# Forget gates as 16 more columns of the first query, key and value projection, h written out tile by tile, and the gate bias on GpSimd's queue

## The chip, the cores and the metric

The kernel runs on one core of a Trainium2 chip. A core has TensorE (PE in the profile; its weight loads are PEld), VectorE (DVE), ScalarE (ACT), GpSimd (POOL) and SyncE (SP, which here only issues DMAs). Each engine works through its own list of instructions in a fixed order; an instruction that has to wait for another engine or for a DMA holds up everything behind it on its engine. The metric is the device time of one execution in microseconds (us).

## The reference, cut to what matters

The program is a decoder trunk for 1024 positions and 1024 features in fp32. It runs a state space layer, a gated feed-forward block, an attention layer, a second feed-forward block and a last norm. The change touches the way into the attention layer:

```python
hn = rmsnorm(h, mix_norm_g[1])
proj = hn @ w_in                       # 1024 x (4*1024 + 16)
q = rmsnorm(proj[..., 0:1024].reshape(.., 16, 64), q_norm_g)
k = rmsnorm(proj[..., 1024:2048].reshape(.., 16, 64), k_norm_g)
v = proj[..., 2048:3072].reshape(.., 16, 64)
gate = proj[..., 3072:4096]
log_f = log_sigmoid(proj[..., 4096:] + b_f)     # 16 columns, one per head
cum = cumsum(log_f over positions)
sc = q @ k^T / 8 + cum[i] - cum[j], causal      # softmax, times v
h = h + (o * sigmoid(gate)) @ w_out
```

## The kernel before, in words

Every fp32 product is three matmuls of split operands (`mm3`, L45 to L51: high times high, high times low, low times high). `split` (L54) makes the two parts: ScalarE copies the high part (L56), then VectorE subtracts it and writes the low part (L57). So a weight goes DMA, tile `raw`, ScalarE, VectorE, and only then can TensorE use all of it. The tile `raw` has two buffers for the whole program (`bufs=2`). A load takes them in turn, and its DMA can't be issued until both halves of the split two loads earlier have read the buffer.

The layer's input is the norm `Norm`. The output projection of the first feed-forward block finishes the eight tiles of h (128 positions each) one after the other (L591 adds the last part to h), and `Norm.tile` scales each to `hn` (squares on ScalarE L173, the factor on VectorE and GpSimd, the scaling on VectorE L200). After four tiles `turn` transposes them: four transposes per 128 features on TensorE (L213) into a PSUM bank, then the high part on ScalarE (L224, into `xh`) and the low part on VectorE (L225, into `xl`). The first half of the positions is turned while the feed-forward block is still running; the second half in `x.finish(bank)` (L952) at the start of `fox`, with three PSUM banks in turn (two named `mt`, one `pv`).

`fox` then does, for heads in 8 pairs:

- It stores all h tiles to DRAM (L953, L954), since the attention needs their memory; they come back for the output projection.
- The forget gates: the last 128 columns of `w_in` go into `raw` (one DMA), the last 32 of them are split (`split_narrow`), and `proj_narrow` (L99, L103) computes them transposed, 32 matmuls 512 columns wide whose weights are the gate columns. ScalarE copies the result (L1156), TensorE transposes it back (L1158, eight times), and VectorE adds the bias `nbf` (L1165, L1167). The bias comes by a DMA on SP's queue (L1149).
- Pair 0's weights: `qkv_w(0)` issues loads 0, 1 and 2, each a `raw` tile that is split into `wqh` and `wql`. Loads 0 and 1 are two DMAs each (L1001, L1002), load 2 is one (L999).
- `softplus` (L904 to L923: three ScalarE operations with two loads of ScalarE's tables, eight VectorE operations) and the running sum over the position tiles (L1173, seven times).
- `in_qkv` for pair 0: for each of 8 position tiles 24 matmuls, 192 in all, 384 columns wide (128 for each of two heads' q with k, and v), evicted by ScalarE (L1019) and split.
- The sums over positions (L1177, L1178), eight transposes of them (L1185), and `fill` for both heads of pair 0, which transposes q and k (L1063) and writes them out with four ScalarE (L1065 to L1068) and two VectorE operations (L1069, L1071) each, four times. The gate projection of pair 0 and the q, k, v projection of pair 1 are handed out beside that.
- The first scores (L1085 to L1089), whose exponential is L1095 on ScalarE; then the loop over pairs, where `fillers` deals out the next pair's projections as work for TensorE between the scores.

The lists are ordered by a scheduler at build time from what the program says and from when tiles become free, and are fixed from then on. `wqh` and `wql` lie in memory that tiles of the norm and of h held before.

Of the kernel before, what the change touches and what calls it, by code (L numbers as in the profile page):

```python
# [17 lines left out]
P = 128  # L18
S = 1024
D = 1024  # L20
# [159 lines left out]
class Norm:  # L180

    def __init__(self, tc, cx, g):
        self.tc, self.cx, self.g = tc, cx, g
# [10 lines left out]
    def tile(self, t, psum):  # L196
        nc, cx = self.tc.nc, self.cx
        hn_t = self.pool.tile([P, D], F32, name="hn")
        r = rstd_of(self.tc, cx, self.small, cx.h[t], hn_t, D, "n")
        nc.vector.tensor_scalar(out=hn_t, in0=cx.h[t], scalar1=r, scalar2=None, op0=ALU.mult)  # L200
        self.hn.append(hn_t)
        if t == 3:
            self.turn(0, psum)
# [36 lines left out]
class BlockNorm(Norm):  # L240
# [3 lines left out]
    def __init__(self, tc, cx, g, h_dram):  # L244
        super().__init__(tc, cx, None)
        self.h_dram = h_dram
        self.gb = self.pool.tile([P, D], F32, name="gb", bufs=1)
        tc.nc.gpsimd.dma_start(out=self.gb, in_=g.unsqueeze(0).broadcast_to([P, D]))
# [685 lines left out]
def fox(tc, cx, x, w_in, b_f, q_norm_g, k_norm_g, w_out, then):  # L934
# [7 lines left out]
    xh, xl = x.xh, x.xl  # L942
    h_dram = [cx.dram.tile([P, D], F32, name=f"h_dram{t}") for t in range(NT)]
    o_dram = [cx.dram.tile([P, S], F32, name=f"o_dram{p}") for p in range(NPR)]

    with ExitStack() as pst:
# [5 lines left out]
        x.finish(bank)  # L952
        for t in range(NT):  # L953
            nc.sync.dma_start(out=h_dram[t], in_=cx.h[t])  # L954
        cx.close_h()
# [32 lines left out]
        def qkv_w(p):  # L988


            wh = qp.tile([P, KD, 3 * P], F32R, name="wqh")
            wl = qp.tile([P, KD, 3 * P], F32R, name="wql")

# [12 lines left out]

        def in_qkv(w, res):

            wh, wl = w
            vt = sp.tile([P, NT, 2, 2, HD], F32R, name="vt", bufs=2)  # L1010
            qn = []
            for t in range(NT):
                hf, tc_ = t // 4, slice((t % 4) * P, (t % 4 + 1) * P)
                ps = ip_ps([P, 3 * P])
                for k in range(KD):
# [13 lines left out]
                eng.tensor_tensor(out=q_, in0=q_, in1=r.unsqueeze(2).broadcast_to([P, 4, HD]), op=ALU.mult)  # L1029
                qn.append(q_.rearrange("p a d -> p (a d)"))  # L1030
            res.update(qn=qn, vt=vt)

# [115 lines left out]
        nbf = sp.tile([P, FH], F32, name="nbf")  # L1148
        nc.sync.dma_start(out=nbf, in_=b_f.broadcast_to([P, FH]))  # L1149
        wf = split_narrow(nc, cx, load_raw(nc, cx, win[:, :, f0:f0 + P]))  # L1150
        fps = small_ps([P, NT, 2, NARROW])
        for hf in range(2):
            ps = ip_ps([P, HF])
            proj_narrow(nc, ps, wf, xh[hf], xl[hf])
            raw = ap_.tile([2 * NARROW, HF], F32, name="ph", bufs=BP)
            nc.scalar.activation(out=raw, in_=ps[0:2 * NARROW], func=AF.Copy)  # L1156
            for c in range(4):
                nc.tensor.transpose(out=fps[:, hf * 4 + c].rearrange("p a h -> p (a h)"), in_=raw[:, c * P:(c + 1) * P],  # L1158
                                    identity=cx.ident[0:2 * NARROW, 0:2 * NARROW])
        res = {}  # L1160
        w, loads = qkv_w(0)
        for f in loads:
            f()
        v = ap_.tile([P, NT, FH], F32, name="g", bufs=1)
        nc.vector.scalar_tensor_tensor(out=v, in0=fps[:, :, 0, FH:2 * FH], scalar=-1.0,  # L1165
                                       in1=nbf.unsqueeze(1).broadcast_to([P, NT, FH]), op0=ALU.mult, op1=ALU.subtract)
        nc.vector.tensor_tensor(out=v, in0=v, in1=fps[:, :, 1, FH:2 * FH], op=ALU.subtract)  # L1167
        sv = ap_.tile([P, NT, FH], F32, name="pl", bufs=BP)
# [158 lines left out]
def trunk_kernel(ctx, tc, x, mix_norm_g, ffn_norm_g,  # L1327
# [4 lines left out]

    def norm(name):
        return lambda: Norm(tc, cx, cx.cols[name])

    def blocks(i):
        return lambda: BlockNorm(tc, cx, ffn_norm_g[i], [cx.dram.tile([P, D], F32, name=f"hf_{i}_{t}") for t in range(NT)])

# [10 lines left out]
    n = ssd(tc, cx, n, ssd_w_in[0], ssd_dt_bias, ssd_a_log, ssd_d, ssd_w_out[0], blocks(0))  # L1349
    n = ffn(tc, cx, 0, n, ffn_w_up, ffn_w_down, norm("mix1"))  # L1350
    n = fox(tc, cx, n, fox_w_in[0], fox_b_f, fox_q_norm_g, fox_k_norm_g, fox_w_out[0], blocks(1))
# [30 lines left out]
```

## Time and profile before

| | us |
|---|---|
| median of 3 runs | 2848.11 (2844.68 to 2848.8) |
| the profiled execution | 2847.88 |
| its span | 2846.2 |
| TensorE busy in it | 2789.2 (98%) |
| VectorE, ScalarE, GpSimd busy | 1983.6, 1439.3, 241.6 |
| mean granted clock of TensorE | 0.998 of full speed |

The span is the time from the first to the last instruction that the profiler saw; 1.7 us of the profiled time lie around it. The stretch in question runs from 1440.5 us (the feed-forward block's last matmul) to about 1511 us (the second scores) of the span. Matmuls overlap, so TensorE's time per matmul is the distance of two starts, not the duration that a row shows.

### The profile page before, as it was taken

What the parts mean: (1) busy time and instruction counts of PE and PEld (TensorE: products, weight loads), DVE (VectorE), ACT (ScalarE), POOL (GpSimd) and SP (SyncE); (2) the same over time, 40 slices, a digit from 0 to 9 for tenths busy, and PEclk for the clock granted to TensorE, in tenths of its full rate; (3) what the DMA queues carried; (4) which work ended last, traced back from release to release, by engine and by line L of the source; (5) the groups of instructions that cost most, each with busy time, mean ns of one, the idle gap of its engine ahead of it and who ended that gap; (6) DMA issues with size and microseconds to landing.
All of it is one profiled execution on the core that took longest, in us unless ns stands there. A gap on an engine that the chain in (4) does not pass through costs nothing. (4 is left out here: it accounts for less than half of the span.)

```text
span 2846.2 us, 37033 instructions
## 1 busy us (share of the span) xinstructions
PE 2789.2 (98%) x14083; PEld 2323.0 (82%) x14083; DVE 1983.6 (70%) x3159; ACT 1439.3 (51%) x2371; POOL 241.6 (8%) x281
## 2 busy tenths in 40 slices
PE   8999999999999999999999999999999999999998
PEld 6888888888778888888888888888877888888887
DVE  6667666666777677667656777776687876776765
ACT  5753754646544444444436666666553544444334
POOL 1000000000100000000023222222200000000000
PEclk9999999999999999999999999999999999999999
DMA  4221212212223333386421111111142233334952
GB/s 138 68 75 52 67 52 64 77 38 75 82 96 97 99 109 104 104 301 207 135 69 29 31 38 38 38 38 38 34 139 102 87 110 111 104 104 138 331 157 103
DMA packets 263394, 275.92 MB, mean 97 GB/s; under 512 B 44162, under 2 KB 193734, under 8 KB 263216
## 3 DMA queue, kind: packets, MB, share of 16 engines
q1 hardware_dynamic: 262448, 271.81, 29.9%
q8 instruction: 111, 1.82, 0.3%
q0 software_dynamic: 752, 1.74, 0.2%
q14 instruction: 67, 0.55, 0.1%
q10 hardware_dynamic: 16, 0.00, 0.0%
HBM read 212.04 MB, written 61.47 MB: 96 GB/s over the span
## 5 line engine op out<-in xcount | busy, mean ns | idle before, releaser
L56 ACT ACTIVATE wh<-raw 128x1024 fp32r<-128x1024 f32 (+2 forms) x162 | 150.2, 929 | 383.0 <-PE fp L50 222.8
L49 PE MATMUL fp<-xh,wh 128*128 128x512 f32 x704 | 274.9, 390 | 0.4 <-DVE h L1318 0.4
L50 PE MATMUL fp<-xl,wh 128*128 128x512 f32 x704 | 274.5, 390 | 0.0
L51 PE MATMUL fp<-xh,wl 128*128 128x512 f32 x704 | 274.3, 390 | 0.0
L57 DVE TENSOR_TENSOR wl<-raw,wh 128x1024 fp32r<-128x1024 f32 (+1 forms) x160 | 171.2, 1070 | 133.8 <-ACT wh L56 133.8
L50 PE MATMUL ip<-xl,wh 128*128 128x512 f32 x640 | 254.8, 398 | 0.0
L49 PE MATMUL ip<-xh,wh 128*128 128x512 f32 x640 | 254.3, 397 | 0.0
L51 PE MATMUL ip<-xh,wl 128*128 128x512 f32 x640 | 253.5, 396 | 0.0
L50 PE MATMUL fp<-wl,ah 128*128 128x512 f32 x616 | 240.5, 390 | 1.0 <-DVE wl L57 0.7
L51 PE MATMUL fp<-wh,al 128*128 128x512 f32 x616 | 239.8, 389 | 0.0
L49 PE MATMUL fp<-wh,ah 128*128 128x512 f32 x616 | 239.0, 390 | 0.0
L478 DVE TENSOR_TENSOR g<-g,fp 128x512 f32<-128x512 f32 x132 | 90.6, 687 | 167.2 <-PE fp L51 167.2
L49 PE MATMUL ip<-wqh,xh 128*128 128x384 f32 x512 | 183.2, 359 | 0.6 <-ACT wqh L56 0.6
L50 PE MATMUL ip<-wql,xh 128*128 128x384 f32 x512 | 174.6, 341 | 1.3 <-DVE wql L57 1.3
L51 PE MATMUL ip<-wqh,xl 128*128 128x384 f32 x512 | 172.9, 338 | 0.0
L56 ACT ACTIVATE ah<-ra 128x1024 fp32r<-128x1024 f32 x84 | 82.6, 988 | 173.7 <-PE fp L50 147.5
L56 ACT ACTIVATE wh<-s 128x1024 fp32r<-128x1024 f32 x88 | 93.5, 1062 | 123.9 <-PE fp L50 120.7
L49 PEld LDWEIGHTS fp<-xh,wh 128*128 128x128 f32 x704 | 132.5, 188 | 27.9 <-ACT wh L56 0.6
L50 PEld LDWEIGHTS fp<-xl,wh 128*128 128x128 f32 x704 | 132.5, 188 | 27.5
L51 PEld LDWEIGHTS fp<-xh,wl 128*128 128x128 f32 x704 | 132.4, 188 | 27.4
L475 ACT ACTIVATE g<-fp 128x512 f32<-128x512 f32 x176 | 103.1, 586 | 101.1 <-PE fp L51 101.1
L694 DVE SCALAR_TENSOR_TENSOR xs<-ip,col,xs 128x511 f32<-128x511 f32 (+2 forms) x120 | 89.1, 745 | 74.1 <-ACT xs L689 73.2
(362 smaller groups left out, 7057.1 us busy)
## 6 DMA issues: line engine op xcount, KB each, us to landing
raw<-in_ffn_w_up_dram SPq DMA_DIRECT2D x88, 512.0 KB, 3.8
a_S<-g SPq DMA_DIRECT2D x88, 256.0 KB, 2.0
raw<-in_ssd_w_in_dram SPq DMA_DIRECT2D x41, 512.0 KB, 3.9
ra<-a_S SPq DMA_DIRECT2D x40, 512.0 KB, 5.9
a_A<-a SPq DMA_DIRECT2D x66, 256.0 KB, 2.1
m<-acs_dram SPq DMA_DIRECT2D x64, 256.0 KB, 3.4
raw<-in_ffn_w_down_dram SPq DMA_DIRECT2D x30, 512.0 KB, 4.9
ra<-a_A SPq DMA_DIRECT2D x30, 512.0 KB, 4.1
```

What stands on the lines that cost most here:

```text
L49: nc.tensor.matmul(out=out, lhsT=lh, rhs=rh, start=start, stop=False, **kw)
L50: nc.tensor.matmul(out=out, lhsT=lh, rhs=rl, start=False, stop=False, **kw)
L51: nc.tensor.matmul(out=out, lhsT=ll, rhs=rh, start=False, stop=stop, **kw)
L56: nc.scalar.activation(out=hi, in_=src, func=AF.Copy)
L57: nc.vector.tensor_tensor(out=lo, in0=src, in1=hi.bitcast(F32), op=ALU.subtract)
L475: nc.scalar.activation(out=to, in_=p, func=AF.Copy)
L478: nc.vector.tensor_tensor(out=to, in0=to, in1=p, op=ALU.add)
L694: nc.vector.scalar_tensor_tensor(out=a[:, sh:], in0=ps[:, 0:HF - sh], scalar=wt, in1=a[:, sh:], op0=ALU.mult, op1=ALU.add)
```

## The change

1. `Norm` gets the DRAM tiles for h and stores each tile of h inside `Norm.tile`, as the feed-forward blocks' norm already did. The loop that stored all eight after `x.finish` is gone.
2. The forget gates have no projection of their own any more. `wqh` and `wql` are 16 columns wider. The same `raw` tile with the last 128 columns of `w_in` is loaded, its last 16 columns are split into columns 384 to 399 of pair 0's `wqh` and `wql`, and then loads 0 to 2 follow. `in_qkv` of pair 0 runs with `more=16`: its 192 matmuls are 400 columns wide, and per position tile one VectorE operation (L1032) adds the bias to the 16 columns. `softplus` and the running sums stand behind `in_qkv` of pair 0 instead of ahead of it. The 32 narrow matmuls, the eight transposes and the two ScalarE copies go.
3. The bias `nbf` is loaded on GpSimd's queue instead of SP's.

```diff
 class Norm, tile():
+        if self.h_dram is not None:
+            nc.sync.dma_start(out=self.h_dram[t], in_=cx.h[t])
 fox():
         x.finish(bank)
-        for t in range(NT):
-            nc.sync.dma_start(out=h_dram[t], in_=cx.h[t])
...
-            wh = qp.tile([P, KD, 3 * P], F32R, name="wqh")
-            wl = qp.tile([P, KD, 3 * P], F32R, name="wql")
+            wh = qp.tile([P, KD, 3 * P + FH], F32R, name="wqh")
+            wl = qp.tile([P, KD, 3 * P + FH], F32R, name="wql")
...
-        def in_qkv(w, res):
+        def in_qkv(w, res, more=0):
-            wh, wl = w
+            wh, wl = (part[:, :, 0:3 * P + more] for part in w)
-                ps = ip_ps([P, 3 * P])
+                ps = ip_ps([P, 3 * P + more])
...
+                if more:
+                    nc.vector.scalar_tensor_tensor(out=res["more"][:, t], in0=ps[:, 3 * P:3 * P + more], scalar=-1.0,
+                                                   in1=nbf, op0=ALU.mult, op1=ALU.subtract)
...
-        nc.sync.dma_start(out=nbf, in_=b_f.broadcast_to([P, FH]))
-        wf = split_narrow(nc, cx, load_raw(nc, cx, win[:, :, f0:f0 + P]))
-        fps = small_ps([P, NT, 2, NARROW])
-        for hf in range(2):
-            ps = ip_ps([P, HF])
-            proj_narrow(nc, ps, wf, xh[hf], xl[hf])
...
+        nc.gpsimd.dma_start(out=nbf, in_=b_f.broadcast_to([P, FH]))
         res = {}
         w, loads = qkv_w(0)
+        raw = load_raw(nc, cx, win[:, :, f0:f0 + P])[:, :, P - FH:P]
+        split(nc, w[0][:, :, 3 * P:3 * P + FH], w[1][:, :, 3 * P:3 * P + FH], raw)
         for f in loads:
             f()
-        v = ap_.tile([P, NT, FH], F32, name="g", bufs=1)
...
+        v = res["more"] = ap_.tile([P, NT, FH], F32, name="g", bufs=1)
+        for _ in in_qkv(w, res, FH):
+            pass
         softplus(...)
         running sums (...)
-        for _ in in_qkv(w, res):
-            pass
```

The lists of the engines are the same up to the second half's turn and again from pair 1's scores on. Three places in between follow. In these rows `mt`, `pv` and `ip` are PSUM tiles, and the waits name the engine or the DMA ring that releases the instruction.

The first place is ScalarE's list at the turn of the second half. Before, the split of load 0 (`wqh<-raw` 128x8x128) stands behind three of the eight evictions, and the narrow columns of the forget gates were split still earlier:

```order
L224 ACTIVATE xh_11446<-mt,col_679 128x512 [waits PE_49] x2
L224 ACTIVATE xh_11446<-pv,col_679 128x512 [waits PE_49]
L56 ACTIVATE wqh<-raw 128x8x128 [waits DMAHW3_49,DMAHW2_49,DMAHW1_49]
L224 ACTIVATE xh_11446<-mt,col_679 128x512 [waits PE_49] x2
L224 ACTIVATE xh_11446<-pv,col_679 128x512 [waits PE_49]
L1156 ACTIVATE ph<-ip 64x512 [waits PE_49]
L56 ACTIVATE wqh<-raw 128x8x128 [waits DMAHW6_49,DMAHW5_49]
```

Now all eight evictions come first (the last rows of them are shown), then the 16 columns and the three loads in a row:

```order
L226 ACTIVATE xh_11454<-pv,col_679 128x512 [waits PE_49]
L226 ACTIVATE xh_11454<-mt,col_679 128x512 [waits PE_49] x2
L56 ACTIVATE wqh<-raw 128x8x16 [waits DMAHW2_49,DMAHW3_49,DMAHW1_49,DVE_49]
L56 ACTIVATE wqh<-raw 128x8x128
L56 ACTIVATE wqh<-raw 128x8x128 [waits DMAHW2_49,DMAHW1_49]
L56 ACTIVATE wqh<-raw 128x8x128 [waits DMAHW3_49]
```

The split that frees the forget gates' `raw` buffer, and the split of load 0, moved behind the last eviction; VectorE's list changed in the same way, with four small operations ahead of the split.

The second place is SP's list. Before, load 1 of pair 0 (L1001, L1002) is issued between the stores of h:

```order
L954 DMA h_dram_11430<-h_9832 128x1024 [waits DVE_49]
L1001 DMA raw<-in_fox_w_in_dram 128x8x64 [waits DMAHW5_49,DVE_49]
L1002 DMA raw<-in_fox_w_in_dram 128x8x64 [waits DMAHW6_49]
L954 DMA h_dram_11431<-h_9833 128x1024 [waits DMAHW7_49,DVE_49]
```

Now it stands behind the last store, and load 2 (L998) directly behind it:

```order
L202 DMA hf_mix_6768<-h_9844 128x1024 [waits DMAHW0_49,DVE_49]
L1000 DMA raw<-in_fox_w_in_dram 128x8x64 [waits DMAHW1_49,DVE_49]
L1001 DMA raw<-in_fox_w_in_dram 128x8x64 [waits DMAHW2_49]
L998 DMA raw<-in_fox_w_in_dram 128x8x128 [waits DMAHW3_49,DVE_49]
```

The stores of h keep their places; what moved is load 1, from between them to behind them, with a wait for VectorE. The bias's DMA left the list.

The third place is TensorE's list where pair 0's projection begins. Before, the transposes of the turn have narrow matmuls (L99, L103) between them, and these go on up to the projection:

```order
L99 MATMUL ip<-xh_11446,wh 64x512 [waits Activation_49]
L1158 MATMUL mt<-ident,ph 128x64 [waits DVE_49]
L1158 MATMUL mt<-ident,ph 128x64 x3
L103 MATMUL ip<-xl_11447,wh 32x512
L49 MATMUL ip<-wqh,xh_11211 128x384 [waits Activation_49]
L49 MATMUL ip<-wqh,xh_11211 128x384
L103 MATMUL ip<-xl_11447,wh 32x512 [waits DVE_49]
```

Now the transposes stand alone and the projection follows them directly:

```order
L215 MATMUL mt<-ident,hn 128x128 [waits DVE_49]
L215 MATMUL mt<-ident,hn 128x128 x3
L49 MATMUL ip<-wqh,xh_11223 128x400 [waits Activation_49]
L49 MATMUL ip<-wqh,xh_11223 128x400 x2
L50 MATMUL ip<-wql,xh_11223 128x400 [waits DVE_49]
```

Nothing stands between the last transposes and the first matmuls that wait for `wqh` and `wql`. Further on, the gate projection of pair 0 (24 matmuls 512 wide) now follows pair 0's projection without a break, and the position sums (L1170, L1171), their transposes (L1178) and the `fill` transposes (L1066) stand among the first matmuls of pair 1's projection, where they stood ahead of and inside the gate projection. Ahead of the second scores (L1085, now L1088, into 128x256) stand 72 of pair 1's 192 matmuls, where 42 stood before; all 24 of the gate projection stand ahead of them in both.

## Rows read from the trace of the kernel before

**Rows 1.** The page's first part: busy time, share of the span, instructions.
```profile
PE 2789.2 (98%) x14083; PEld 2323.0 (82%) x14083; DVE 1983.6 (70%) x3159; ACT 1439.3 (51%) x2371; POOL 241.6 (8%) x281
```

**Rows 2.** Windows: stretch, length; busy PE, PEld, DVE, ACT, POOL; clock, DMA share, GB/s.
```profile
1440.50:1456.20 15.70, 13.29 (x76) 8.14 (x74) 12.15 (x21) 10.10 (x18) 2.49 (x5) 1.00 0.41 127
...
1489.60:1512.00 22.40, 18.67 (x105) 15.33 (x104) 15.03 (x27) 19.03 (x31) 6.80 (x4) 1.00 0.31 71
```

**Rows 3.** Timeline of PE: start, us, engine, line, tiles, shapes, count, [idle before].
```profile
1443.17 0.39 PE L99 MATMUL ip<-xh,wh 128*64 128x512 f32 x1
1443.40 0.40 PE L103 MATMUL ip<-xl,wh 128*32 128x512 f32 x1
...
1455.81 0.46 PE L1158 MATMUL mt<-ident,ph 64*128 64x64 f32 x4 [0.68 <-ACT ph L1156]
1456.20 0.45 PE L49 MATMUL ip<-wqh,xh 128*128 128x384 f32 x1
...
1489.07 0.34 PE L51 MATMUL ip<-wqh,xl 128*128 128x384 f32 x1
```

**Rows 4.** Timeline of ACT at the second half's turn and behind it.
```profile
1444.73 1.27 ACT L224 ACTIVATE xh<-mt,col 128x512 fp32r<-128x512 f32 x2 [2.08 <-PE mt L213]
...
1452.94 1.06 ACT L56 ACTIVATE wqh<-raw 128x1024 fp32r<-128x1024 f32 x1 [1.14 <-DMA raw<-in_fox_w_in_dram]
```

**Rows 5.** Timeline of DVE from the first half's turn to the running sums.
```profile
1420.45 5.35 DVE L225 SCALAR_TENSOR_TENSOR xl<-fp,col,xh 128x512 fp32r<-128x512 f32 x8
...
1433.06 0.42 DVE L57 TENSOR_TENSOR wh<-raw,wh 128x256 fp32r<-128x256 f32 x1 [4.49 <-ACT wh L56]
...
1445.45 1.41 DVE L225 SCALAR_TENSOR_TENSOR xl<-mt,col,xh 128x512 fp32r<-128x512 f32 x2 [1.14 <-ACT xh L224]
...
1454.50 1.23 DVE L57 TENSOR_TENSOR wql<-raw,wqh 128x1024 fp32r<-128x1024 f32 x1
...
1463.81 2.17 DVE L1173 TENSOR_TENSOR pl<-pl 128x16 f32<-128x16 f32 x7
```

**Rows 6.** Timeline of SP's queue: when loads 1 and 2 are issued.
```profile
1433.51 0.38 SPq L1001 DMA_DIRECT2D raw<-in_fox_w_in_dram  x1
1433.94 0.58 SPq L1002 DMA_DIRECT2D raw<-in_fox_w_in_dram  x1
...
1448.80 0.38 SPq L999 DMA_DIRECT2D raw<-in_fox_w_in_dram  x1
```

**Rows 7.** Line L1002's DMAs: time from issue to landing.
```profile
DMA to landing us min/median/max: 3.8/3.9/5.3
```

**Rows 8.** Timeline of ACT behind pair 0's projection.
```profile
1489.44 0.38 ACT L1019 ACTIVATE qn<-ip 128x256 f32<-128x256 f32 x1 [3.61 <-PE ip L51]
...
1489.88 2.01 ACT L56 ACTIVATE wqh<-raw 128x1024 fp32r<-128x1024 f32 x2
1491.78 1.07 ACT L56 ACTIVATE k<-mt 32x512 fp32r<-32x512 f32 x2
...
1496.34 1.06 ACT L56 ACTIVATE wqh<-raw 128x1024 fp32r<-128x1024 f32 x1 [0.87 <-DMA raw<-in_fox_w_in_dram]
1497.63 0.68 ACT L1065 ACTIVATE q<-mt,gqk 64x512 fp32r<-64x512 f32 x1 [0.23 <-PE mt L1063]
...
1508.80 1.28 ACT L1095 ACT_TABLE_LOAD   x1
1510.10 0.37 ACT L1095 ACTIVATE e<-sc,mx 128x128 f32<-128x128 f32 x1
```

**Rows 9.** Timeline of PE at pair 1's first matmuls and the second scores.
```profile
1498.72 0.45 PE L50 MATMUL ip<-wql,xh 128*128 128x384 f32 x1
...
1510.61 0.39 PE L1085 MATMUL sc<-k,q 128*128 128x256 f32 x1 [2.14 <-ACT e L1095]
```

**Rows 10.** Windows near the span's start, columns as in rows 2.
```profile
21.00:23.00 2.00, 1.28 (x10) 0.92 (x10) 1.55 (x3) 2.00 (x6) 1.33 (x2) 1.00 0.00 0
...
25.00:27.00 2.00, 2.00 (x8) 1.48 (x7) 1.87 (x3) 1.79 (x4) 0.00 (x0) 0.50 0.04 11
27.00:29.00 2.00, 2.00 (x11) 1.51 (x10) 1.65 (x3) 1.40 (x4) 0.00 (x0) 0.70 0.93 251
```

More of the change, by code (lines that the diff above doesn't have):

```diff
@@ L180, with __init__ @@
 class Norm:
-    def __init__(self, tc, cx, g):
-        self.tc, self.cx, self.g = tc, cx, g
+    def __init__(self, tc, cx, g, h_dram=None):
+        self.tc, self.cx, self.g, self.h_dram = tc, cx, g, h_dram
         self.st = ExitStack()
@@ L244, in __init__ @@
     def __init__(self, tc, cx, g, h_dram):
-        super().__init__(tc, cx, None)
-        self.h_dram = h_dram
+        super().__init__(tc, cx, None, h_dram)
         self.gb = self.pool.tile([P, D], F32, name="gb", bufs=1)
@@ L942, in fox @@
     xh, xl = x.xh, x.xl
-    h_dram = [cx.dram.tile([P, D], F32, name=f"h_dram{t}") for t in range(NT)]
+    h_dram = x.h_dram
     o_dram = [cx.dram.tile([P, S], F32, name=f"o_dram{p}") for p in range(NPR)]
@@ L1148, in fox @@
         nbf = sp.tile([P, FH], F32, name="nbf")
-        nc.sync.dma_start(out=nbf, in_=b_f.broadcast_to([P, FH]))
-        wf = split_narrow(nc, cx, load_raw(nc, cx, win[:, :, f0:f0 + P]))
-        fps = small_ps([P, NT, 2, NARROW])
-        for hf in range(2):
-            ps = ip_ps([P, HF])
-            proj_narrow(nc, ps, wf, xh[hf], xl[hf])
[L1155 to L1159, printed above, removed]
+        nc.gpsimd.dma_start(out=nbf, in_=b_f.broadcast_to([P, FH]))
         res = {}
         w, loads = qkv_w(0)
+        raw = load_raw(nc, cx, win[:, :, f0:f0 + P])[:, :, P - FH:P]
+        split(nc, w[0][:, :, 3 * P:3 * P + FH], w[1][:, :, 3 * P:3 * P + FH], raw)
         for f in loads:
             f()
-        v = ap_.tile([P, NT, FH], F32, name="g", bufs=1)
-        nc.vector.scalar_tensor_tensor(out=v, in0=fps[:, :, 0, FH:2 * FH], scalar=-1.0,
-                                       in1=nbf.unsqueeze(1).broadcast_to([P, NT, FH]), op0=ALU.mult, op1=ALU.subtract)
-        nc.vector.tensor_tensor(out=v, in0=v, in1=fps[:, :, 1, FH:2 * FH], op=ALU.subtract)
+        v = res["more"] = ap_.tile([P, NT, FH], F32, name="g", bufs=1)
+        for _ in in_qkv(w, res, FH):
+            pass
         sv = ap_.tile([P, NT, FH], F32, name="pl", bufs=BP)
@@ L1331, in trunk_kernel, with h_dram, norm @@
     cx = Ctx()
-    def norm(name):
-        return lambda: Norm(tc, cx, cx.cols[name])
+    def h_dram(i):
+        return [cx.dram.tile([P, D], F32, name=f"hf_{i}_{t}") for t in range(NT)]
+    def norm(name, *h):
+        return lambda: Norm(tc, cx, cx.cols[name], *h)
     def blocks(i):
-        return lambda: BlockNorm(tc, cx, ffn_norm_g[i], [cx.dram.tile([P, D], F32, name=f"hf_{i}_{t}") for t in range(NT)])
+        return lambda: BlockNorm(tc, cx, ffn_norm_g[i], h_dram(i))
     w_in = ssd_w_in[0].rearrange("(k p) c -> p k c", p=P)
@@ L1349, in trunk_kernel @@
     n = ssd(tc, cx, n, ssd_w_in[0], ssd_dt_bias, ssd_a_log, ssd_d, ssd_w_out[0], blocks(0))
-    n = ffn(tc, cx, 0, n, ffn_w_up, ffn_w_down, norm("mix1"))
+    n = ffn(tc, cx, 0, n, ffn_w_up, ffn_w_down, norm("mix1", h_dram("mix")))
     n = fox(tc, cx, n, fox_w_in[0], fox_b_f, fox_q_norm_g, fox_k_norm_g, fox_w_out[0], blocks(1))
```

## The prediction

> **What bounds the kernel now.** I read the page first: TensorE is busy for 2789.2 of 2846.2 us [rows 1], so a change pays or costs what it does to TensorE's list, its work and its waits. Then the windows around the start of the attention. From the feed-forward block's last matmul to pair 0's steady projection (1440.5 to 1456.2) TensorE is busy for 13.29 of 15.70 us; from the projection's end to the second scores (1489.6 to 1512.0) for 18.67 of 22.40 [rows 2]. Between them it has no gap. These two stretches are where the change acts, and 2.4 and 3.7 us of idle time is all there is to win in them beside work that goes. Then I read each engine's timeline in both, with one question: what is TensorE fed by? In the first, it is the splits of pair 0's weights: the last waits 1.14 us on ScalarE for its DMA [rows 4] and ends on VectorE at 1455.7 [rows 5]; the projection takes its step at 1456.20 [rows 3]. Meanwhile TensorE has the narrow gate matmuls to do, so that the wait hardly shows. In the second, the largest wait is for the first exponential on ScalarE, 2.14 us [rows 9].
>
> **The work that goes and comes.** Narrow matmuls follow each other by 0.23 us (1443.17, 1443.40) [rows 3]: 32 of them are 7.4 us. The eight transposes behind them, four within 0.46 us [rows 3], are 0.8 us at most. An estimate of the columns added: pair 0's matmuls of 384 columns are spaced (1489.07 - 1456.20)/189 = 0.174 us, the 512 wide ones 0.23 [rows 3]; that is 0.0004 us a column, so 16 columns are 0.007 us and 192 matmuls 1.3 us. TensorE's work falls by 8.2 - 1.3 = 6.9 us. If it were never kept waiting, that would be the gain.
>
> **What keeps it waiting now.** The bound is the two `raw` buffers. In the order of loads the forget gates take one, load 0 the other, load 1 the first again, load 2 the second. Before, the forget gates' columns were split into a tile that was free, and VectorE was done with it at 1433.06 + 0.42 [rows 5]; load 1 left at 1433.51 [rows 6], during the feed-forward block. After, the 16 columns go into `wqh` and `wql`, and ScalarE's and VectorE's lists have that split behind all eight evictions of the second half's turn. So load 1 waits for the turn. Step by step, on the clock of the trace of before:
>
> - The turn's evictions start on VectorE at 1445.45; eight took 5.35 us in the first half's turn [rows 5]. That is 1450.8; with three PSUM banks in turn I take 1451.4.
> - Four small operations and the split of the 16 columns: the narrow split was twice as wide and took 0.42 us [rows 5], so I put the five at 0.9 us together (bounds 0.4 and 2.1): 1452.3. Load 1's first DMA is issued, its second 0.43 us later (1433.51, 1433.94) [rows 6], at 1452.7. It lands 3.9 us on [rows 7]: 1456.6.
> - Load 0 is split meanwhile, which lets load 2 go at about 1453.5; it lands at 1457.6, so it is not what ends last.
> - ScalarE splits loads 1 and 2 with 1.06 us each [rows 4]: 1457.7 and 1458.8. VectorE with 1.23 each [rows 5]: 1458.9 and 1460.2. The first matmul that needs `wql` starts at 1460.2, where before it stood at about 1456.5, one step behind the row at 1456.20 [rows 3].
>
> So the projection's bulk is 3.7 us later although 8.2 us of work ahead of it is gone, and TensorE stands idle from about 1450 to 1459. With the 1.3 us of added columns the projection ends 5.0 us late.
>
> **What is late next.** `softplus` and the running sums lay beside the projection before, at no cost (running sums until 1466 [rows 5]). Now they lie behind it, ahead of the position sums, the k splits and the `fill`. ScalarE carries that chain. Its last eviction was at 1489.44 and load 2 of pair 1 landed at 1496.34 [rows 8]; 5.0 us later is 1501.4. The third split 1.06: 1502.4. Then a table load of 1.28 and the logarithm with two VectorE operations, all on 128 columns like the first exponential with its 0.37 [rows 8], 1.0 together: 1504.7. The seven running sums 2.17 [rows 5]: 1506.9. The position sums, their transposes and the k splits: before, from the projection's last matmul at 1489.07 [rows 3] to the end of the first two k splits at 1492.85 [rows 8] were 3.8 us, and two more are 1.07: 1511.8. The 16 evictions of `fill` ran without a gap before, from 1497.63 to the table load at 1508.80 [rows 8], 11.2 us, and have one more eviction (0.38) among them now: 1523.4. The table load of the exponential was at 1508.80: that is 14.6 us later, and with it the second scores, before at 1510.61 [rows 9].
>
> TensorE does more in that time: by the lists, 72 of pair 1's 192 matmuls stand ahead of the second scores, where 42 stood before. 30 by 0.174 are 5.2 us of work done early. What is lost at the second scores is 14.6 - 5.2 = 9.4 us. The bounds: below, if TensorE finds the work again that it lacked, the 5.0 us of the projection's end stays; above, if the scores of pair 0 have nothing to lie beside for want of those 30 matmuls, all 14.6 us stay. I take 9.4: in the stretches behind, TensorE was the engine that others waited for. From pair 1 on the lists are equal, and nothing there gives time back.
>
> **The clock.** At the start of the program, after a stretch in which TensorE was busy 1.28 of 2.00 us with transposes and waits, the granted clock fell to 0.50 (1.2 GHz) and 0.70 in the next slices [rows 10]; what that costs is (1.00 - 0.50) * 2 + (1.00 - 0.70) * 2 = 1.6 us of full speed work. The turn before had 2.4 us of waiting in 15.7 and kept 1.00 [rows 2]. The 9 us gap stands nearer to the first. A fall would begin in the gap, where it costs nothing, and I put in half, 0.8 us (bounds 0 and 1.6). The Trainium skill, "TensorE: Matmul & The Clock Gate", section "Why this matters for your kernels", advises against gaps in TensorE's work between bursts of matmuls, since the clock falls back to its lower level behind them; by that rule the whole 1.6 us would be due and the time 2858.9, and the trace's first slices agree with it.
>
> **At no cost.** The stores of h keep their places in SP's list, and nothing that TensorE needs stood behind them but load 1. The bias on GpSimd's queue is needed at the first projection tile's end, some 4 us behind the point where the projection starts; if it were late, VectorE alone would wait. Eight small VectorE operations (L1032) lie beside the projection, in which VectorE has little to do. Each of the three, without its cover, is under 1 us.
>
> **The sum.** 2847.88 (profiled, 0.2 below the median of 2848.11) + 9.4 + 0.8 = 2858.1 us. Its own range is 2847.9 + 5.0 to 2847.9 + 14.6 + 1.6: 2853 to 2864.
>
> **Rivals.**
>
> - Faster: the waits are hidden, and the removed work pays. It needs load 1 to land by the time the turn ends, so that its splits run at 1452 and the projection starts at about 1454 to 1456 with 400 columns; then the end moves by -6.9 to 2841, or less. For it speaks that the gate matmuls were TensorE's own work, 98% of a span; against it the split's place in both lists and the buffer count. It decides from a landing of load 1 ahead of 1452. 0.10.
> - No change: the projection is late, but the chain behind it is shorter than I added up, since table loads and small operations run while ScalarE would wait, and TensorE's early 30 matmuls are all worth their time. 5.0 less the 2.1 us of waiting for the exponential that was there anyway is +3, 2851. For it speaks that TensorE idled 3.7 us in that stretch before [rows 2]; against it that ScalarE was busy 19.03 of those 22.40 us already and gets more. 0.20.
> - Slower by more: pair 0's scores lack the 30 matmuls, all 14.6 us stay, and the clock falls in the first gap and again at the second scores: 14.6 + 2 * 1.6, 2866. For it speaks that the order is fixed and can't deal the work out anew; against it that TensorE waited for little in pair 0's loop. 0.12.
>
> My forecast has 0.58. The range is 2846 to 2865: at the lower end it leaves out the faster case and little of the one without change, at the upper the last. A measurement of this kernel tells about 0.2% from no change, 5.7 us. Faster by more is the first rival, 0.10; within it are the second and the lowest part of my forecast's range (under 2853.8), 0.22; slower is the rest, 0.68.
>
> **What would show it.** In the profile after: L1000 issued between 1451 and 1454; a gap of TensorE of 8 to 10 us behind the turn's transposes, ended by `wqh` or by `wql`; the first matmul on `wql` near 1460, the projection's end near 1494; matmuls of 400 columns 0.18 us apart; a wait of 2 us or more for pair 1's third split; the exponential's table load near 1523 and TensorE waiting for it; from pair 1 on, the same distance to the times of before. It is wrong if load 1 leaves ahead of the evictions' end, or if the distance at the first scores shrinks again in the pairs behind.

## The result: 0.63% slower, and where the time went

The kernel after takes 2864.9 us (median of 4 runs, 2862.9 to 2865.5) against 2847.2 of the kernel before (4 runs, 2844.7 to 2848.8): a ratio of 1.0063 (95% interval [1.0047, 1.0079]), some 18 us. The prediction was 2858.1, with a range of 2846 to 2865. The measured time lies at the upper edge of that range; the loss, 17.7 us, is more than the 17.1 us that the edge allows over the 2847.9 from which it was reckoned. The direction was right, and so were the two places of the loss. The cause given for the first place was not, and the clock and the credit for work done early were mis-sized.

TensorE has 40 matmuls and transposes less to do: its busy time is 0.7 us less than in [rows 1], although a part of it now runs at a lower clock, and the span is 16.5 us longer.

```profile
PE 2788.5 (97%) x14043; PEld 2326.8 (81%) x14043; DVE 1982.7 (69%) x3165; ACT 1439.8 (50%) x2369; POOL 241.6 (8%) x282
```

To find the place, both traces are cut at the same five events: the feed-forward block's last matmul, pair 0's first matmul on `wql`, its last projection matmul, the second scores, and the load of the exponential's table for pair 1. Four events in the trace after (start, us, engine, line, tiles, shapes, count, idle before); the waits of 9.83 and 3.23 us answer to the 0.68 us in [rows 3] and the 2.14 us in [rows 9]:

```profile
1439.46 0.39 PE L51 MATMUL fp<-wh,al 128*128 128x512 f32 x1
...
1459.51 1.37 PE L49 MATMUL ip<-wqh,xh 128*128 128x400 f32 x3 [9.83 <-ACT wqh L56]
1460.77 0.70 PE L50 MATMUL ip<-wql,xh 128*128 128x400 f32 x1
...
1497.26 0.34 PE L50 MATMUL ip<-wql,xh 128*128 128x400 f32 x1
1497.44 0.34 PE L51 MATMUL ip<-wqh,xl 128*128 128x400 f32 x1
...
1505.82 0.62 PE L49 MATMUL ip<-wqh,xh 128*128 128x384 f32 x2 [2.41 <-ACT wqh L56]
...
1529.23 0.39 PE L1088 MATMUL sc<-k,q 128*128 128x256 f32 x1 [3.23 <-ACT e L1098]
```

The windows between the events, first of before, then of after (stretch, length; busy PE, PEld, DVE, ACT, POOL; granted clock, DMA share, GB/s):

```profile
1440.34:1456.49 16.15, 13.74 (x77) 8.43 (x76) 12.33 (x22) 10.55 (x18) 2.49 (x5) 1.00 0.41 128
1456.49:1489.07 32.58, 32.58 (x189) 32.58 (x189) 12.34 (x41) 7.90 (x20) 15.71 (x21) 1.00 0.15 33
1489.07:1510.61 21.54, 17.81 (x100) 14.51 (x99) 14.10 (x23) 18.32 (x29) 6.19 (x3) 1.00 0.33 74
1510.61:1575.93 65.32, 63.23 (x387) 55.00 (x387) 46.82 (x103) 37.74 (x82) 19.68 (x24) 1.00 0.10 25
```

```profile
1439.46:1460.77 21.31, 7.79 (x37) 5.63 (x35) 12.64 (x22) 9.89 (x16) 4.10 (x6) 0.72 0.37 99
1460.77:1497.44 36.67, 36.67 (x190) 36.62 (x189) 7.65 (x29) 4.92 (x15) 15.67 (x21) 0.93 0.19 42
1497.44:1529.23 31.79, 24.80 (x129) 21.07 (x128) 18.87 (x43) 22.53 (x36) 6.44 (x6) 0.95 0.22 50
1529.23:1593.35 64.12, 59.93 (x357) 51.66 (x357) 46.09 (x101) 37.15 (x81) 18.09 (x21) 0.97 0.10 26
```

The differences of the lengths are +5.16, +4.09, +10.25 and -1.20: together +18.3 us. In the first window TensorE now idles 13.5 us instead of 2.4; in the third 7.0 instead of 3.7. After pair 1 the distance of the two traces stays near that: on the spans' own clocks the table loads of pairs 1 and 7 lie 17.4 and 18.5 us apart. The spans differ by less, 16.5 us, because two stretches that the change leaves alone were shorter in the trace after: 0.9 us up to the first event and 2 us behind the attention layer.

ScalarE in the trace after, at the turn and behind the projection, answers to [rows 4, 8]: load 1's split waits 5.25 us for its DMA, the third split of pair 1 waits 2.62, the k splits wait 4.89 for the sums, and the table load that stood at 1508.80 comes at 1527.43.

```profile
1450.31 1.25 ACT L56 ACTIVATE wqh<-raw 128x128 fp32r<-128x128 f32 x2
1456.81 1.06 ACT L56 ACTIVATE wqh<-raw 128x1024 fp32r<-128x1024 f32 x1 [5.25 <-DMA raw<-in_fox_w_in_dram]
1458.40 1.06 ACT L56 ACTIVATE wqh<-raw 128x1024 fp32r<-128x1024 f32 x1 [0.54 <-DMA raw<-in_fox_w_in_dram]
...
1500.48 1.28 ACT L915 ACT_TABLE_LOAD   x1
...
1504.71 1.06 ACT L56 ACTIVATE wqh<-raw 128x1024 fp32r<-128x1024 f32 x1 [2.62 <-DMA raw<-in_fox_w_in_dram]
1505.78 1.28 ACT L921 ACT_TABLE_LOAD   x1
...
1512.27 1.07 ACT L56 ACTIVATE k<-mt 32x512 fp32r<-32x512 f32 x2 [4.89 <-PE mt L1178]
...
1527.43 1.28 ACT L1098 ACT_TABLE_LOAD   x1
```

SP's queue and VectorE answer to [rows 6, 5]. Load 1 leaves behind the split of the 16 columns (grouped with load 0's in one row, `x2`), load 2 1.1 us later:

```profile
1452.09 0.38 SPq L1000 DMA_DIRECT2D raw<-in_fox_w_in_dram  x1
1452.53 0.58 SPq L1001 DMA_DIRECT2D raw<-in_fox_w_in_dram  x1
1453.22 0.84 SPq L998 DMA_DIRECT2D raw<-in_fox_w_in_dram  x1
```

```profile
1444.68 1.41 DVE L227 SCALAR_TENSOR_TENSOR xl<-mt,col,xh 128x512 fp32r<-128x512 f32 x2 [1.21 <-ACT xh L226]
...
1449.87 1.41 DVE L227 SCALAR_TENSOR_TENSOR xl<-mt,col,xh 128x512 fp32r<-128x512 f32 x2
...
1451.84 1.36 DVE L57 TENSOR_TENSOR wql<-raw,wqh 128x128 fp32r<-128x128 f32 x2
...
1459.49 1.23 DVE L57 TENSOR_TENSOR wql<-raw,wqh 128x1024 fp32r<-128x1024 f32 x1 [0.37 <-ACT wqh L56]
```

The granted clock, which before was 1.00 in all four windows, falls three times after. Windows of 2 us (columns as above): at half speed (1.2 GHz) when the projection starts, and again behind the waits of 2.41 and 3.23 us.

```profile
1462.00:1464.00 2.00, 2.00 (x8) 1.98 (x7) 0.00 (x0) 0.24 (x1) 0.00 (x0) 0.50 1.14 268
1464.00:1466.00 2.00, 2.00 (x8) 1.98 (x7) 1.15 (x1) 0.82 (x1) 0.00 (x0) 0.53 0.52 95
1466.00:1468.00 2.00, 2.00 (x13) 2.00 (x12) 0.08 (x1) 0.38 (x2) 0.00 (x0) 1.00 0.25 57
1506.00:1508.00 2.00, 1.36 (x5) 0.93 (x4) 1.57 (x4) 1.37 (x2) 0.00 (x0) 0.71 0.44 83
1508.00:1510.00 2.00, 2.00 (x9) 1.91 (x8) 1.41 (x10) 0.00 (x0) 0.00 (x0) 0.50 0.87 198
...
1530.00:1532.00 2.00, 1.48 (x6) 1.11 (x6) 1.61 (x7) 0.80 (x4) 0.78 (x2) 0.68 0.00 0
1532.00:1534.00 2.00, 2.00 (x9) 1.90 (x8) 1.18 (x5) 0.55 (x2) 1.15 (x2) 0.50 0.00 0
```

### The profile page after: what moved, and what is told of

It reads as the page before. It is cut to its first block, busy times and chain, and to the rows that moved or that the text cites. A ratio compares the mean times of both kernels' runs of the same rounds, so it can differ in the third digit from the quotient of the medians.

```text
span 2862.7 us, 36970 instructions
## 1 busy us (share of the span) xinstructions
PE 2788.5 (97%) x14043; PEld 2326.8 (81%) x14043; DVE 1982.7 (69%) x3165; ACT 1439.8 (50%) x2369; POOL 241.6 (8%) x282
## 5 line engine op out<-in xcount | busy, mean ns | idle before, releaser
L49 PE MATMUL ip<-wqh,xh 128*128 128x384 f32 (+1 forms) x512 | 185.4, 364 | 12.2 <-ACT wqh L56 12.2
L50 PE MATMUL ip<-wql,xh 128*128 128x384 f32 (+1 forms) x512 | 178.0, 348 | 1.9 <-DVE wql L57 1.9
L51 PE MATMUL ip<-wqh,xl 128*128 128x384 f32 (+1 forms) x512 | 176.1, 344 | 0.0
```

The source lines that it names most:

```text
L49: nc.tensor.matmul(out=out, lhsT=lh, rhs=rh, start=start, stop=False, **kw)
L50: nc.tensor.matmul(out=out, lhsT=lh, rhs=rl, start=False, stop=False, **kw)
L51: nc.tensor.matmul(out=out, lhsT=ll, rhs=rh, start=False, stop=stop, **kw)
```

## The experiments

The theory to test: the change loses at two places, the late loads of pair 0's weights and the softplus chain behind the projection, and the clock adds to both. All times are medians with the ratio to the kernel before on the same chip (2847.5 to 2848.6 us there). The first step means pair 0's first matmul on `wql`. The table gives, for each kernel that was cut at the five events, the four windows' lengths less those of before; it is worked out as above.

| kernel | to the first `wql` | projection | to the second scores | to pair 1 | sum |
|---|---|---|---|---|---|
| after | +5.2 | +4.1 | +10.3 | -1.2 | +18.3 |
| before, chain late | 0.0 | 0.0 | +13.0 | -1.4 | +11.6 |
| after, `qn` in a pool of its own | 0.0 | +2.7 | +11.1 | -0.7 | +13.1 |
| after, all loads free | -0.6 | +3.1 | +11.2 | -0.6 | +13.1 |
| after, `fill` ahead of the sums | +5.5 | +3.3 | +2.2 | +0.5 | +11.4 |
| after, free loads and `fill` ahead | +0.3 | +4.6 | +2.2 | +0.5 | +7.5 |
| after, TensorE kept busy in the first gap | +5.5 | +1.8 | +10.5 | -1.2 | +16.6 |
| the same, and 12 more behind the projection | +5.2 | +2.9 | +9.3 | -1.2 | +16.1 |

**Stores and bias alone.** The kernel before with parts 1 and 3 of the change; the narrow projection stays.

```diff
 Norm.tile():
+            nc.sync.dma_start(out=self.h_dram[t], in_=cx.h[t])
 fox():
-        for t in range(NT):
-            nc.sync.dma_start(out=h_dram[t], in_=cx.h[t])
-        nc.sync.dma_start(out=nbf, ...)
+        nc.gpsimd.dma_start(out=nbf, ...)
```

> The kernel before with parts 1 and 3 of the change alone: h is stored inside the norm, the bias is loaded on GpSimd's queue, the forget gates keep their narrow projection. Theory (all of the loss is part 2): within 2 us of before, and the projection of pair 0 takes its step at the same place, near 1456. Rival (the stores or the bias's queue cost something): 3 us or more over before, with a later start of the projection.

2847.4 us, ratio 0.9999 [0.9989, 1.0008]. These two parts cost nothing; all of the loss is in part 2.

**The chain alone, late.** The kernel before; the bias, softplus and running sums stand behind `in_qkv`, tied to its last tile by a factor made from it.

```diff
+        for _ in in_qkv(w, res):
+            pass
+        neg = ...  # res["r"][:, 0:1] * 0 - 1, of the last tile
-        nc.vector.scalar_tensor_tensor(out=v, ..., scalar=-1.0, ...)
+        nc.vector.scalar_tensor_tensor(out=v, ..., scalar=neg, ...)
         softplus(...); running sums
-        for _ in in_qkv(w, res):
-            pass
```

> The kernel before with its narrow gate projection and its loads, but the bias, softplus and the running sums made to depend on the last tile of pair 0's projection, so that they lie behind it as in the changed kernel. Theory (two separate losses, and this chain is one): the projection starts and ends as before (1489); the table load for the first exponential comes 30 us behind its end, as in the changed kernel, in place of 19.7; the granted clock falls near the two waits; 6 to 9 us over before, 2853 to 2856. Rival (the late loads explain all, the chain is covered by the 30 matmuls done early): within 2 us of before.

2859.8 us, ratio 1.0043 [1.0027, 1.0060]. Windows of this kernel, from the projection's start on:

```profile
1454.15:1486.73 32.58, 32.58 (x189) 32.58 (x189) 7.40 (x22) 4.50 (x15) 15.68 (x21) 1.00 0.15 33
1486.73:1521.28 34.55, 25.76 (x130) 22.08 (x129) 19.39 (x45) 22.51 (x36) 6.43 (x6) 0.88 0.20 46
1521.28:1585.16 63.88, 60.38 (x357) 52.04 (x357) 45.94 (x101) 37.08 (x81) 17.16 (x21) 0.96 0.10 26
```

The projection takes exactly as long as before, and 11.6 us are lost behind it: the chain's place by itself is the larger part of the loss, and more than the 6 to 9 us expected. Up to (1.00 - 0.88) * 34.55 = 4.1 us of it is the clock. TensorE does 30 matmuls more in the second window, yet the third is only 1.4 us shorter.

**The 16 columns split early.** The kernel after, but the columns are loaded and split ahead of the turn into a free weight tile, and GpSimd copies them into `wqh` and `wql`.

```diff
+        raw = load_raw(...)[:, :, P - FH:P]; split(nc, *x.few, raw)   # ahead of x.finish(bank)
         x.finish(bank)
-        split(nc, w[0][:, :, 3 * P:3 * P + FH], w[1][:, :, 3 * P:3 * P + FH], raw)
+        nc.gpsimd.tensor_copy(out=part[:, :, 3 * P:3 * P + FH], in_=few)   # high and low
```

> The changed kernel, but the forget gates' raw tile is split early into a tile of its own (as before the change) and GpSimd copies the 16 columns into wqh and wql; so load 1 leaves near 1433 again. Theory (the place of load 0's split behind the evictions is what delays, through load 2): load 2 still leaves near 1453 and lands near 1457, the first matmul on wql is 1 to 2 us earlier than the changed kernel's 1460.8, the whole 2862 to 2865. Rival (what the prediction argued: load 1's wait alone makes the projection late): the projection starts near 1456.5 and the whole is near 2859.

2865.1 us, ratio 1.0057 [1.0042, 1.0072]. Load 1 leaves at 1432.91 as it did before, and it helps hardly at all:

```profile
1432.91 0.38 SPq L1004 DMA_DIRECT2D raw<-in_fox_w_in_dram  x1
...
1453.88 0.38 SPq L1002 DMA_DIRECT2D raw<-in_fox_w_in_dram  x1
```

Load 2 (L1002) still leaves at 1453.88, because load 0's split, which frees its buffer, is behind the turn too; the first step still waits 8.74 us. So load 1's wait for the split of the 16 columns, the prediction's reason, is not what makes the projection late.

**`qn` in a pool of its own.** What holds every split behind the turn? The pool with `wqh`, `wql` and the eight `qn` has 32 KB per partition before (12 + 12 + 8), as much as the eight tiles of h whose place it takes (8 * 4 KB). By these sizes it lay in h's memory alone. With 16 columns more it has 33 KB, so its first tile, `wqh`, reaches 1 KB into the norm's memory, which the turn's last transposes still read. The edit makes the pool small again.

```diff
+        qnp = qst.enter_context(tc.tile_pool(name="a_qn", ...))
-                q_ = qp.tile([P, 4, HD], F32, name="qn", bufs=8)
+                q_ = qnp.tile([P, 4, HD], F32, name="qn", bufs=8)
```

> The changed kernel with qn in a pool of its own behind that of wqh and wql. In the changed kernel the pool of wqh, wql and qn is 33 KB per partition, where the eight h tiles ahead of it were 32 KB; so its first tile, wqh, reaches into the norm's memory, which the turn's last transposes read. Here wqh and wql lie in h's memory alone. Theory (that reach is what puts the splits behind all evictions): the split of the 16 columns and of load 0 stand between the evictions again, load 1 leaves near 1448 in place of 1452, the first matmul on wql stands near 1456 to 1458 in place of 1460.8, the clock falls less, the whole is 3 to 6 us shorter than the changed kernel's 2865. Rival (what the prediction said, two raw buffers and the order of loads): load 1 and load 2 stay behind one another, less than 2 us gained.

2861.3 us, ratio 1.0047 [1.0032, 1.0062]. The loads leave between the evictions again, and the first step stands at 1454.30, 16.19 us behind the feed-forward block as before (16.15):

```profile
1445.63 0.38 SPq L1001 DMA_DIRECT2D raw<-in_fox_w_in_dram  x1
1446.07 0.57 SPq L1002 DMA_DIRECT2D raw<-in_fox_w_in_dram  x1
1446.90 0.79 SPq L999 DMA_DIRECT2D raw<-in_fox_w_in_dram  x1
```

This names the cause: the size of the pool, not the two `raw` buffers. Those are as in the kernel after, and load 1 still leaves 12 us later than before (1445.63 against 1433.51), at no cost in the first window. The edit gives back 5.2 us and not more: the first window has its old length again and is no shorter, though 8.2 us of narrow matmuls and transposes are gone.

**All loads free.** As the last, and the gates' `raw` and load 2 take free weight tiles, so that no load waits for a buffer.

```diff
-        raw = load_raw(nc, cx, win[:, :, f0:f0 + P])[:, :, P - FH:P]
+        raw = cx.wp.tile([P, D], F32, name="fraw", tag="wl")...; nc.sync.dma_start(out=raw, ...)
-                raw = cx.wp.tile([P, D], F32, name="raw", bufs=2)...
+                kind = dict(name="raw2", tag="wh") if p == 0 and i == 2 else dict(name="raw", bufs=2)
```

> As pool_order, and the forget gates' raw tile and load 2 take buffers of the split weights (tags wl and wh) in place of the two raw buffers, so that all loads of pair 0 are there before the turn. This takes the first loss away and leaves softplus behind the projection. Theory (two losses that add up): no gap of more than 2 to 3 us ahead of the projection, no fall of the clock there, the projection ends 8 us ahead of the changed kernel's 1497.4; the rest, 9 to 11 us over before, is the softplus chain: 2856 to 2859. Rival (one loss hides the other, the chain only hurts because the projection is late): within 4 us of before.

2856.7 us, ratio 1.0031 [1.0019, 1.0043]. The first step is not earlier: with the loads there, the step on `wql` waits for VectorE.

```profile
1451.15 1.37 PE L49 MATMUL ip<-wqh,xh 128*128 128x400 f32 x3
1455.22 0.70 PE L50 MATMUL ip<-wql,xh 128*128 128x400 f32 x1 [2.70 <-DVE wql L57]
```

VectorE is almost without a break there (busy for 4.59 of the 5 us from 1450 to 1455): eight evictions and the splits, 1.23 us a load, end at about 1455 whatever the loads do. So the narrow matmuls lay beside work of VectorE that remains, and to remove them could win nothing here. The clock was expected not to fall there and was at 0.50 from 1445 to 1458. At pair 1 this kernel is no better than the last; that its time is lower, and within the 2856 to 2859 expected, is luck: it comes from later pairs, where 0.48 us a pair come back for the reason shown at the last experiment.

**`fill` ahead of the sums.** The kernel after with pair 1's loads, then softplus, then `fill`, then the position sums and k splits, so that ScalarE has the 16 evictions to do while the chain runs.

```diff
+        gate = dict(w=gate_w(3 * FD)); w, loads = qkv_w(1); [f() for f in loads]
         softplus(...); running sums
+        for a in range(2): for hf in range(2): fill(0, a, res["qn"], hf)
         position sums, transposes, k splits
-        for a in range(2): for hf in range(2): fill(0, a, res["qn"], hf)
```

> The changed kernel with only the order behind the projection changed: pair 1's loads, then softplus, then the q and k fills, and the position sums and k splits last, so that ScalarE does the fills while VectorE does softplus (the first write of q2 takes its zeros from another finite tile). Theory (the chain on ScalarE behind the projection is the second loss): the first exponential's table load comes 21 to 24 us behind the projection's end in place of 30, the whole 4 to 8 us shorter than the changed kernel's 2865. Rival (TensorE's lack of other work there is what counts, not the chain): less than 2 us gained.

2858.6 us, ratio 1.0040 [1.0026, 1.0054]. The third window shrinks from 31.79 to 23.74 us with a clock of 1.00. It gives back 6.9 us: the wait on the chain was real, and it is a matter of order (of pair 1's loads and of `fill` together; the run does not separate the two).

**Both.** Free loads and `fill` ahead together.

```diff
+        "all loads free", with qn in its own pool
+        "fill ahead of the sums"
```

> loads_free and late_k together: the forget gates as 16 columns of the projection without either loss. Theory: the 6.9 us of TensorE's work that the change removes begins to pay; 2843 to 2850, about as before or a little faster. Rival (other waits take over, as the k splits being last on ScalarE's list): 2853 or more.

2854.1 us (10 runs), ratio 1.0024 [1.0014, 1.0033]: still slower than before, against the expectation. The windows:

```profile
1439.57:1456.01 16.44, 7.31 (x38) 5.01 (x36) 13.51 (x23) 10.48 (x17) 5.47 (x8) 0.88 0.44 127
1456.01:1493.16 37.15, 37.15 (x188) 37.15 (x189) 7.49 (x29) 3.87 (x14) 15.71 (x21) 0.92 0.07 15
1493.16:1516.90 23.74, 18.34 (x100) 14.75 (x99) 18.12 (x42) 21.71 (x35) 2.59 (x2) 1.00 0.29 67
1516.90:1582.69 65.79, 63.08 (x386) 55.16 (x386) 46.98 (x102) 38.06 (x81) 20.23 (x23) 1.00 0.10 25
```

The two gains nearly add: 5.2 and 6.9 us apart, 10.8 together. What is left is 4.6 us in the projection, of which (1.00 - 0.92) * 37.15 = 3.0 are the clock and 1.6 the columns, and 2.2 of the chain. TensorE idles 9.1 us in the first window where it had matmuls to do before, and starts the projection at half speed.

**TensorE kept busy in the gap.** The kernel after with 30 matmuls of 512 columns, whose result nothing uses, ahead of the projection.

```diff
+        for k in range(30):
+            nc.tensor.matmul(out=warm, lhsT=xh[1][:, KD - 1, 0:P], rhs=xh[1][:, KD - 1, :], ...)
         v = res["more"] = ...
```

> The changed kernel with 30 extra matmuls, 512 wide, on the last part of xh into a PSUM bank that nothing reads, between the turn's last eviction and the projection: TensorE works in the gap, nothing waits for them. Theory (the clock is a cost of its own): the granted clock stays at 1.00 (or back at it) from 1452 to 1466, the projection ends 2 to 3 us ahead of the changed kernel's 1497.4, and the whole is 2 to 3 us shorter, near 2862, although there is more work. Rival (the waits explain all, the clock next to nothing): the projection ends where it did or later, 2865 or more.

2862.4 us, ratio 1.0050 [1.0036, 1.0065]. The projection starts no earlier, and runs in 34.36 us at a clock of 1.00 instead of 36.67 at 0.93:

```profile
1459.52:1493.88 34.36, 34.36 (x188) 34.36 (x189) 7.64 (x29) 4.92 (x15) 15.67 (x21) 1.00 0.19 45
```

So the first fall costs 2.3 us, and the columns are the 1.8 that stay over 32.58. The whole is 2.5 us shorter than the kernel after, as expected, but the two intervals overlap.

**And 12 more behind the projection**, against the second fall.

```diff
+        for k in range(12):
+            nc.tensor.matmul(out=cold, ...)   # ahead of pair 1's projection
```

> The changed kernel with the 30 extra matmuls in the first gap as before, and 12 more of them between pair 0's projection and its gate projection, where TensorE has to wait 3 us for pair 1's third load anyway. Theory (each fall of the clock costs about 1.6 us of its own): no fall behind the second wait either, about 1.5 us off the distance from the turn to pair 1's first scores against the run with 30 alone; the whole near 2861. Rival (the chain on ScalarE sets that time, TensorE's clock there is covered): no difference to the run with 30 alone, or later.

2865.0 us, ratio 1.0061 [1.0045, 1.0076]. The clock held at 1.00 from 1500 to 1515, although the 12 matmuls take 2.9 us themselves, and the window to the second scores is 1.2 us shorter than with the 30 alone (30.79 against 32.01 us). That is the second fall's price at its place. The first fall came back in this run (clock 0.67 from 1460 to 1465, behind 30 matmuls that ended at 1458), so by the distance to pair 1 the kernel is only 0.5 us ahead of the last, and its time doesn't show it.

**Both, with 18 idle matmuls in the gap.** Their result is not used.

```diff
+        for k in range(18):
+            nc.tensor.matmul(out=cold, ...)   # in the kernel "both", ahead of pair 0's projection
```

> The version without either loss, with 18 extra matmuls of 512 columns between the turn's last eviction and the first matmul on wql, where TensorE waits 4.1 us for VectorE's splits. Theory (VectorE's turn and splits bound the projection's start at 1455 to 1456 with or without the narrow matmuls, and those kept the clock up): the projection starts as late as without the extra matmuls, runs at full clock and ends 2 to 3 us earlier; the whole 1.5 to 3 us shorter than the 2854 of that version, so still not faster than before. Rival (the extra matmuls are in the way): 2854 or more.

2855.9 us, ratio 1.0028 [1.0017, 1.0038], not better than "both". The clock was at 0.50 already when they began (1450.93), they took 6.77 us for it. The projection then ran in 34.61 us instead of 37.15, but it started later and ended no earlier: 54.2 us behind the feed-forward block's last matmul, against 53.6 in "both". A miss: they stood too late to help.

**The order of `fill` without the change.** The kernel before with parts 1 and 3 (the first experiment) and `fill` ahead of the position sums; the narrow projection stays, and softplus beside the projection.

```diff
         for _ in in_qkv(w, res):
             pass
+        pair 1's loads; fill(0, a, res["qn"], hf) four times
         position sums, transposes, k splits
-        fill(0, a, res["qn"], hf) four times
```

> The kernel before with parts 1 and 3 of the change, the narrow gate projection kept, and only the order behind pair 0's projection changed: pair 1's loads and the q and k fills first, the position sums and k splits last, as in late_k. Theory (before, ScalarE idled 2 to 3 us between the k splits ahead of the fills): the first exponential's table load comes 17 to 18 us behind the projection's end in place of 19.7 and the whole is 1 to 3 us shorter than before, 2845 to 2847. Rival (the k splits behind the fills only move the wait): 2848 or more.

2844.1 us (11 runs), ratio 0.9987 [0.9978, 0.9996]: shorter than both kernels, by little. The gain isn't where it was looked for. The table load at the first scores is 1.45 us earlier (1507.35 against 1508.80), but at pair 1 the traces stand level again; then each of five pairs wins 0.63 us, 3.2 in all. The new order is not what wins them: "`fill` ahead of the sums" has that order and no such gain, and "all loads free" has the old order and a gain of the same kind. In the two kernels that win, one GpSimd operation per pair takes 1.01 us instead of 1.97. The first of the five, with VectorE's split beside it, before:

```profile
1634.88 1.23 DVE L57 TENSOR_TENSOR wql<-raw,wqh 128x1024 fp32r<-128x1024 f32 x1
1634.99 1.97 POOL L1028 TENSOR_TENSOR r<-r,mhalf 128x4 f32<-128x4 f32 x1 [2.23 <-DVE r L1027]
```

and in this run:

```profile
1635.00 1.01 POOL L1027 TENSOR_TENSOR r<-r,mhalf 128x4 f32<-128x4 f32 x1 [2.23 <-DVE r L1026]
1635.21 1.23 DVE L57 TENSOR_TENSOR wql<-raw,wqh 128x1024 fp32r<-128x1024 f32 x1 [0.29 <-issue]
```

Where the split starts 0.11 to 0.13 us ahead, the operation takes 1.97 us (all five pairs of the kernels before, after, "`qn` in a pool of its own" and "both"); where it starts 0.21 to 0.23 us behind, 1.01 (all five pairs of these two). The transposes of the next `fill` hang on it: TensorE waits 0.97 us for them before and 0.31 here. Why the split starts later in two of the kernels is open.

## Why the prediction was too low, step by step

- **Work.** Right: matmuls of 400 columns start 0.18 us apart (1497.26, 1497.44), as forecast, and at full clock the 16 columns cost 1.8 us (34.36 - 32.58) against 1.3. That the narrow work gains nothing by going was right as well; what it lay beside is VectorE's work, which the prediction did not say.
- **The loads.** The cause was wrong, and that the times came out is in part luck. Load 1 was forecast at 1452.3 and left at 1452.09, the gap was to be 8 to 10 us and is 9.83, the step on `wql` was to be near 1460 and is at 1460.77. But this trace's turn is 0.88 us earlier (1439.46 against 1440.34), so that measured from there all of it is late, and the window grew by 5.2 us where 3.7 were forecast. VectorE's evictions took 6.6 us instead of 6.0 (1444.68 to 1451.28), and load 2 landed 5.2 us behind its issue (1453.22, 1458.40) instead of 4.1: "it is not what ends last" failed. The step read the lists' order rightly and explained it by `raw`; the pool's size explains it.
- **The chain.** From the projection's end to the second scores 9.6 us were forecast (14.6 - 5.0), and 10.25 measured. Without the clock's share, (1.00 - 0.95) * 31.79 = 1.6 by the granted clock and 1.2 by the run with 12 more matmuls, it would be 8.7 to 9.1: the sum was right to 1 us.
- **The 30 matmuls.** This term was mis-sized. They were credited with all of 5.2 us; the last window is only 1.20 us shorter. The clock took (1.00 - 0.97) * 64.12 = 1.9 of the rest, and waits the other 2.1: TensorE idles 4.19 us there instead of 2.09. The waits of TensorE in that window of the trace after (line waited for: us in total, times, longest); before, the same two lines, L1117 and L1063 there, had 0.2 and 0.3 us:

```profile
PE mt L1120 <- DVE e L1101: 1.4, 3, 0.7
...
PE mt L1066 <- DVE pl L57: 1.0, 1, 1.0
```

  The 1.2 us more in the first line are the scores' own: it fits that they lack those matmuls to stand beside them, as the last rival had said, though no run separates it. The 0.7 us more in the second line are not: they go with the GpSimd operation of the last experiment, which takes 1.95 us here and 1.01 before.
- **The clock.** This term was mis-sized most: 0.8 us forecast. By the granted clock three falls cost 2.6 (0.07 * 36.67), 1.6 and 1.9, together 6.1 us; experiments put the first at 2.3 and the second at 1.2, the third none did. The forecast knew the first place and took half of it, because "a fall would begin in the gap, where it costs nothing"; but in this trace the clock did not come back in the gap: it was at 0.50 or little over it until 1466, through more than 5 us of the projection. The other two stand behind waits of 2.41 and 3.23 us that the forecast had as well, and gave no clock. Its price of 1.6 us was read at the start of the program [rows 10], where the fall came behind waits of 0.7 and 0.8 us (on `hn`, at 22.35 and 24.71), so it was no price of a long gap. The Trainium skill, "TensorE: Matmul & The Clock Gate", section "Why this matters for your kernels", advises against idle gaps between bursts of matmuls. The trace agrees at the gaps of 9.83 and 3.23 us; the wait of 2.41 us is shorter than the gaps that the section names, and the clock fell there too. By that rule the price of a fall had to be charged at both gaps and not once.

Of the 8.1 us between +18.3 and the forecast's +10.2 the clock is 5.3, the waits that ate the credit for the 30 matmuls 2.1, the later start 1.5 and the columns 0.2, less 1.0 that the chain was shorter. With the experiments' prices for the first two falls the clock is 4.6, the columns 0.5 and the chain 0.6 shorter. The last rival, at 2866 and with a chance of 0.12, came nearest, with two falls for three and without the part of the 30 matmuls' credit that was paid.

## What to carry to other kernels

Work that fills a wait is free, and taking it away buys nothing until what it waited beside is gone too; it can cost the clock. When a tile grows, look at what its pool overlays: 1 KB too much moved every split of a stage behind the last reader. A chain that lay beside a long stage should not be put behind it without moving something else into its place, and each new wait of TensorE should be asked what a fall of the clock behind it would cost: here it fell behind 2.41 us, and before, behind the 2.14 us ahead of the second scores, it did not. A gain of a few us is to be looked for in the trace at the place of the edit; that of the last experiment lay elsewhere.

## What had not been expected of the hardware

The clock fell while TensorE still had transposes of the turn to do: in the trace after it was 0.50 from 1446 to 1448, ahead of the gap, where the turn with narrow matmuls among its transposes kept 1.00. TensorE's waits in that turn were 0.78, 1.50 and 1.41 us; before, with narrow matmuls in between, 0.78 and 0.34. In the run with free loads it fell in the same part of the turn, among waits of the same lengths. Behind the wait of 2.41 us, which followed a full stretch, it fell too. One GpSimd operation took twice as long when a split on VectorE had started 0.1 us ahead of it, and five of them are the whole gain of the last experiment.

And the trace after loses some 0.17 us more with each pair from 1 to 7 (17.4 to 18.5), though the lists are equal there; the first two experiments, whose tiles are those of before, don't. It is in TensorE's own work: from the table load of pair 2 to that of pair 3 it is busy for 76.55 us before and 76.75 after, with 472 matmuls in both. In the four kernels with `wqh` of 384 columns it is 76.5 to 76.6 us, in the nine with 400 it is 76.7 to 76.8, although both read 384 columns there. Why that takes longer is open.
